# A roll along the columns of an 8192 x 8192 float32 matrix: dealing the long row pieces to the DMA engines in another order

## The chip, the core and the metric

The kernel runs on one core of a Trainium2 chip. The metric is device time in microseconds (us), the median of several executions. The core has five compute engines, which hardly matter here, and 16 DMA engines, which do all the work that counts. DMAs are put on queues by SP (SyncE), by ACT (ScalarE) and by POOL (GpSimd). Each queue feeds the same 16 DMA engines.

## The reference

```python
def setup_inputs():
    return {"x": np.random.randn(8192, 8192).astype(np.float32), "shift": 100}

def reference(x, shift):
    return np.roll(x, shift, axis=1)
```

Each row of the output is the same row of the input, turned by 100 elements: `out[r, 100:] = x[r, :8092]` and `out[r, :100] = x[r, 8092:]`. Nothing is computed; 268.4 MB are read from device memory and 268.4 MB are written to it. A row is 8192 x 4 B = 32 KiB, and rows follow one another in memory without gaps, so "rows apart" times 32 KiB gives the distance in memory.

## The kernel before

With `s = 100`, the kernel sets `a = 128` (the shift rounded up to 128 elements, so that the long writes start on a 512 B boundary of the output) and `g = a - s = 28`. Each output row is made of two pieces.

**Long pieces** (L28 to L31). Columns 128 to 8191 of the output come straight from columns 28 to 8091 of the input, 8064 elements = 32256 B of each row, by DMAs from device memory to device memory. The 8192 rows are cut into `n_chunks = 16` blocks of 512 consecutive rows, and one DMA moves one block. Even blocks are issued by SP, odd ones by ACT, so eight DMAs go on each of the two queues, in the order of the loop. The 16 completion signals of each DMA come from the 16 DMA engines; an engine has 512 / 16 = 32 rows of each DMA. Within a DMA the access pattern is 512 x 8064, and nothing in the source says which 32 rows go to which engine. That is what the change is about.

**Heads** (L48 to L70). Columns 0 to 127 of the output need the last 100 elements of the input row and its first 28. These are fetched into SBUF by POOL's DMAs, put together, and written out as 512 B pieces. There are `n_st = 2` stages of 4096 rows; in each of them partition `p` holds 32 consecutive rows, numbered by `j` (8) and `q` (`Q = 4`), so that one DMA for one `q` takes rows that are 4 apart. For `q` = 1, 2, 3 the 128 elements that straddle the border between the previous row and this one are read as one piece (L61); they hold the 28 elements at this row's start, and the 100 at the end of the row before. L62 and L65 fetch what this leaves out, VectorE copies (L63, L66) shift the pieces to their rows in `h`, and four DMAs for each stage (L70) write `h` out. All of POOL's DMAs are on POOL's queue.

The three queues start together and share the 16 DMA engines. The kernel ends when the last DMA has landed. Its end is waited for on SP (shown at L101).

Of the kernel before, what the change touches and what calls it, by code (L numbers as in the profile page):

```python
# [1 line left out]

# [4 lines left out]


@with_exitstack
def kernel(  # L10
    ctx: ExitStack,
    tc: tile.TileContext,
    x: bass.AP,
    shift: int,
    out: bass.AP,
):
    nc = tc.nc
    n_rows, n_cols = x.shape
    s = shift % n_cols
    a = -(-s // 128) * 128  # L20
    g = a - s
    P = nc.NUM_PARTITIONS
    engines = [nc.sync, nc.scalar]
    n_chunks = 16
    rows = n_rows // n_chunks


    for i in range(n_chunks):  # L28
        r = slice(i * rows, (i + 1) * rows)
        if a < n_cols:  # L30
            engines[i % 2].dma_start(out=out[r, a:], in_=x[r, g:n_cols - s])  # L31
    if a == 0:
        return


    if a > 512:
        for i in range(n_chunks):
            r = slice(i * rows, (i + 1) * rows)
            nc.gpsimd.dma_start(out=out[r, :s], in_=x[r, n_cols - s:])
            if g > 0:  # L40
                nc.gpsimd.dma_start(out=out[r, s:a], in_=x[r, :g])
        return

    Q, J = 4, 8  # L48
    n_st = n_rows // (P * Q * J)
    reads = ctx.enter_context(tc.tile_pool(name="reads", bufs=n_st))  # L50
    heads = ctx.enter_context(tc.tile_pool(name="heads", bufs=n_st))
    xt = x.rearrange("(k p j q) c -> k q p j c", q=Q, j=J, p=P)
    ot = out.rearrange("(k p j q) c -> k q p j c", q=Q, j=J, p=P)
    tiles = []
    for k in range(n_st):
        t = reads.tile([P, Q - 1, J, a], x.dtype)
        h = heads.tile([P, Q, J, a], x.dtype)
        for q in range(1, Q):
            lead = bass.AP(tensor=x.tensor, offset=(k * P * J * Q + q) * n_cols - s,
                           ap=[[J * Q * n_cols, P], [Q * n_cols, J], [1, a]])  # L60
            nc.gpsimd.dma_start(out=t[:, q - 1], in_=lead)  # L61
        nc.gpsimd.dma_start(out=h[:, Q - 1, :, :s], in_=xt[k, Q - 1, :, :, n_cols - s:])  # L62
        nc.vector.tensor_copy(h[:, :Q - 1, :, :s], t[:, :, :, :s])  # L63
        if g > 0:
            nc.gpsimd.dma_start(out=h[:, 0, :, s:], in_=xt[k, 0, :, :, :g])  # L65
            nc.vector.tensor_copy(h[:, 1:, :, s:], t[:, :, :, s:])  # L66
        tiles.append(h)
    for k, h in enumerate(tiles):
        for q in range(Q):
            nc.gpsimd.dma_start(out=ot[k, q, :, :, :a], in_=h[:, q])  # L70


# [1 line left out]
_INS = ['x', 'shift']  # L74
_OUTS = [((8192, 8192), 'float32')]

_NUMBERS = {'shift': 100}


# [26 lines left out]
```

## Time and profile before

| what | value |
|---|---|
| median of 7 runs | 835.09 us (828.78 to 840.04) |
| the profiled execution | 835.53 us |
| its span, first to last instruction | 833.7 us |
| POOL busy / VectorE busy | 16.1 us (2%) / 3.7 us (0%) |
| moved by DMA | 272.63 MB, mean 327 GB/s |
| device memory read and written | 268.44 MB each, 644 GB/s together over the span |
| long pieces, queues q1 and q10 | 4224 packets each, 132.12 MB each |
| heads, queue q0 | 2336 packets, 8.39 MB |

The profile shows instructions of the compute engines, and packets of the DMA engines by queue. The hardware queues q1 and q10 are the ones that SP and ACT issue on, q0 is POOL's. A share of a queue is the time that its packets took, divided by 16 engines times the span. In the 4224 packets of each long queue there are 4096 rows of 32256 B, and 8 x 16 completion signals, so a row is one packet. The view of stretches of the span gives for each stretch the busy share of the 16 DMA engines and the GB/s that they moved.

### The profile page before, as it was taken

Reading aid. Unit: us, or ns where it says so; the run is one execution under the profiler, and the core shown is the slowest. Engines: PE = TensorE matmul, PEld = TensorE weight load, DVE = VectorE, ACT = ScalarE, POOL = GpSimd, SP = SyncE. Lnnn points to the kernel's source line nnn. Section 1 sums busy time; section 2 is a strip of 40 time slices with the busy share of each in tenths; the row PEclk is TensorE's granted clock in tenths of the full one; section 3 lists DMA queues with packets and bytes.
Section 4 is the critical chain, followed back from the end, with each engine's and each line's share of the span. In section 5 each row is a group of like instructions: output and inputs, shape, how many; then the busy total and the mean of one; then the engine's idle time right before and its main releaser. Section 6 shows DMA issues by size and latency. Waiting matters only on the chain. (4 is left out here: it accounts for less than half of the span.)

```text
span 833.7 us, 93 instructions
## 1 busy us (share of the span) xinstructions
DVE 3.7 (0%) x4; POOL 16.1 (2%) x22
## 2 busy tenths in 40 slices
DVE  0000000000000000000000000000000000000000
POOL 3000001000010000000000000000000000000000
DMA  9999999999999999999999999999999999999996
GB/s 297 323 335 330 335 334 324 340 324 339 334 331 339 338 329 338 342 335 340 331 332 345 328 330 319 325 334 322 325 331 320 327 328 320 316 328 316 327 322 248
DMA packets 10784, 272.63 MB, mean 327 GB/s; under 512 B 544, under 2 KB 544, under 8 KB 2592
## 3 DMA queue, kind: packets, MB, share of 16 engines
q10 hardware_dynamic: 4224, 132.12, 47.4%
q1 hardware_dynamic: 4224, 132.12, 46.4%
q0 software_dynamic: 2336, 8.39, 4.8%
HBM read 268.44 MB, written 268.44 MB: 644 GB/s over the span
## 5 line engine op out<-in xcount | busy, mean ns | idle before, releaser
L70 POOL DMA_DIRECT2D out_dram<-h x8 | 6.9, 957 | 172.3 <-DMA h<-in_x_dram 145.6
L61 POOL DMA_DIRECT2D t<-in_x_dram x6 | 5.4, 912 | 0.8 <-PEq L101 0.8
L63 DVE COPY h<-t 128x2400 f32<-128x2400 f32 x2 | 2.8, 1410 | 213.2 <-DMA t<-in_x_dram 213.2
L62 POOL DMA_DIRECT2D h<-in_x_dram x2 | 1.8, 884 | 30.6 <-DMA t<-in_x_dram 30.6
L65 POOL DMA_DIRECT2D h<-in_x_dram x2 | 1.8, 884 | 29.2 <-DMA t<-in_x_dram 29.2
L66 DVE COPY h<-t 128x672 f32<-128x672 f32 x2 | 1.0, 503 | 0.0
L87 POOL MEMSET const-float32-0.0<- 128x1 f32 x1 | 0.1, 99 | 0.2 <-issue 0.2
L87 POOL MEMSET const-bfloat16-1.0<- 128x1 bf16 x1 | 0.1, 102 | 0.0
L87 POOL MEMSET const-float32-1.0<- 128x1 f32 x1 | 0.1, 99 | 0.0
L87 POOL MEMSET const-uint8-127<- 128x1 uint8 x1 | 0.1, 99 | 0.0
## 6 DMA issues: line engine op xcount, KB each, us to landing
out_dram<-in_x_dram SPq DMA_DIRECT2D x8, 16128.0 KB, 409.7
out_dram<-in_x_dram ACTq DMA_DIRECT2D x8, 16128.0 KB, 409.0
out_dram<-h POOLq DMA_DIRECT2D x8, 512.0 KB, 185.5
t<-in_x_dram POOLq DMA_DIRECT2D x6, 512.0 KB, 123.6
h<-in_x_dram POOLq DMA_DIRECT2D x2, 400.0 KB, 155.4
h<-in_x_dram POOLq DMA_DIRECT2D x2, 112.0 KB, 149.7
```

Source lines behind the costliest of these rows:

```text
L61: nc.gpsimd.dma_start(out=t[:, q - 1], in_=lead)
L62: nc.gpsimd.dma_start(out=h[:, Q - 1, :, :s], in_=xt[k, Q - 1, :, :, n_cols - s:])
L63: nc.vector.tensor_copy(h[:, :Q - 1, :, :s], t[:, :, :, :s])
L65: nc.gpsimd.dma_start(out=h[:, 0, :, s:], in_=xt[k, 0, :, :, :g])
L66: nc.vector.tensor_copy(h[:, 1:, :, s:], t[:, :, :, s:])
L70: nc.gpsimd.dma_start(out=ot[k, q, :, :, :a], in_=h[:, q])
L87: nc = _bacc.Bacc("TRN2", target_bir_lowering=False, num_devices=1)
```

## The change

The 16 long DMAs stay 16, eight for each of SP and ACT, 512 rows each, and the same bytes go to the same places. Which rows are in a DMA, and how its access pattern is laid out, is different. A row's number is read as `64 c + 4 e + j`, with `e` from 0 to 15 and `j` from 0 to 3. A DMA takes one `j`, all 16 `e`, and 32 consecutive values of `c`. Its pattern has `e` as first dimension: 16 x 32 x 8064. One engine then has one value of `e`: rows that step by 64 (2 MiB), while the next engine's rows lie 4 further on (128 KiB). SP issues `j` = 0 and 2, ACT `j` = 1 and 3. A quarter of the matrix (2048 rows) is covered by four DMAs before the next quarter begins. The heads' code is not touched; its DMAs took rows 4 apart already.

```diff
-    for i in range(n_chunks):
-        r = slice(i * rows, (i + 1) * rows)
-        if a < n_cols:
-            engines[i % 2].dma_start(out=out[r, a:], in_=x[r, g:n_cols - s])
+    xm = x.rearrange("(c e j) w -> j e c w", e=16, j=4)
+    om = out.rearrange("(c e j) w -> j e c w", e=16, j=4)
+    depth = n_rows // 64 // 4
+    for c in range(4):
+        for j in range(4):
+            if a < n_cols:
+                cs = slice(c * depth, (c + 1) * depth)
+                engines[j % 2].dma_start(out=om[j, :, cs, a:], in_=xm[j, :, cs, g:n_cols - s])
```

## The prediction, made before the changed kernel was run

> **What bounds the kernel now.** I read the busy rows of the page first, then the share of each DMA queue, then the stretches of the span, and last the waits of SP's queue. The first two views, from the page:
>
> ```profile
> DMA  9999999999999999999999999999999999999996
> GB/s 297 323 335 330 335 334 324 340 324 339 334 331 339 338 329 338 342 335 340 331 332 345 328 330 319 325 334 322 325 331 320 327 328 320 316 328 316 327 322 248
> ...
> q10 hardware_dynamic: 4224, 132.12, 47.4%
> q1 hardware_dynamic: 4224, 132.12, 46.4%
> q0 software_dynamic: 2336, 8.39, 4.8%
> HBM read 268.44 MB, written 268.44 MB: 644 GB/s over the span
> ```
>
> All 16 DMA engines are at work from the first slice to the last; the compute engines are idle. The shares give the price of a row: (47.4% + 46.4%) x 16 x 833.7 us / 8192 rows = 1.527 us for each row if the completion packets were free, counted on 32256 B. They are free (4 B each, 9 ns in the packet records). So a row costs an engine about 1.53 us, or 21.1 GB/s. The packet records give the same picture in detail: the fastest rows took 1.193 us (27.0 GB/s, 433 GB/s over 16 engines), half took over 1.47 to 1.52 us, one in twenty over 2.0 us. A row that nothing holds up takes 22% less than the mean. Something that the engines share holds them back: the memory, or the way to it.
>
> The stretches, eight of about one pair of long DMAs each (columns: length, VectorE and POOL busy, clock, DMA share, GB/s):
>
> ```profile
> 0.00:104.00 104.00, 1.83 (x2) 9.14 (x14) 1.00 0.98 323
> 312.00:416.00 104.00, 0.00 (x0) 0.00 (x0) 1.00 1.00 337
> 520.00:624.00 104.00, 0.00 (x0) 0.00 (x0) 1.00 1.00 326
> 624.00:728.00 104.00, 0.00 (x0) 0.00 (x0) 1.00 1.00 324
> 728.00:833.00 105.00, 0.00 (x0) 0.00 (x0) 1.00 0.93 310
> ```
>
> The second half moves long rows alone, and is the cleanest place: DMA share 1.00, 324 to 326 GB/s. It holds still for 200 us, so this is a steady limit and no start-up effect. In the last stretch the share is 0.93: engines run out of rows before the slowest does, and 7% of 105 us = 7 us are lost there.
>
> ```profile
> SPq L101 <- DMA out_dram<-in_x_dram: 324.4, 4, 102.9
> SPq L31 <- DMA out_dram<-in_x_dram: 47.8, 4, 17.0
> ```
>
> Issuing is not late: SP put its last long DMA in at 424.7 us, and then only waited for landings, 324.4 us in all. The median long DMA lands 409 us after its issue. About four are always queued on each ring.
>
> **The change part by part.**
>
> *Issue.* 16 long DMAs before and after, 512 rows each, 32 for each engine, the same order of SP and ACT. The instruction order on SP, ACT and POOL is the same; only the pattern turns from 512 x 8064 into 16 x 32 x 8064. If making the longer pattern costs more, the four queued DMAs (some 400 us of work) cover it. Bare price with that cover gone: the shortest issue in the trace took 0.58 us, so 8 x 0.58 = 5 us for each queue. I take 0.
>
> *Heads.* Untouched: 18 DMAs on POOL, last issued at 249 us. They hold 4.8% of the engines, 40 us of the span, wherever they run. Only their neighbours change. With the long rows out of their way or in it, they could move by some us against a slack of over 300 us to the end. I take 0.
>
> *No bytes, packets or waits change.* Everything hangs on one term: 93.8% of 833.7 = 782 us in which 16 engines copy rows. What can change is the 1.53 us of a row, since neighbouring engines read and write 128 KiB apart and not 1 MiB (if an engine had 32 consecutive rows before), an engine's next row is 2 MiB on and not 32 KiB, and the two rings work on adjacent rows and not 16 MiB apart. All 32 rows that are under way lie in 2 MiB of the input and 2 MiB of the output.
>
> The trace does not show the address of a row's packet, so this is bounded. *From below*: with no contention, 1.193/1.527 of 782 = 611 us, which saves 171. That is not reachable by an order of rows if memory itself is the limit: the Trainium skill's "HBM Reference", section Specifications, gives about 716 GB/s for the memory that a pair of cores shares, and the trace shows 644. By row alone I would allow 171 us; by the page at most (1 - 644/716) x 833.7 = 84 us, an estimate. I let the page set this end, as the steady 1.00 share at 324 GB/s (650 GB/s of reads and writes) agrees with a shared limit. *From above*: the rule that bears on the change is in "DMA: Bandwidth & Descriptors", section Latency and other measured facts, the row on HBM row pitch at large powers of two: copies between tensors with a row pitch of 512 KiB ran at 207 GB/s in each direction, of 2 MiB at 164, of 4 MiB at 103. It speaks against the change if the pitch that matters is that of one engine's list, which becomes 2 MiB: 782 x (207/164 - 1) = +205 us, an estimate. It speaks for the change if what matters is the distance between engines, which falls from 1 MiB to 128 KiB. The trace has 322 GB/s in each direction at what I take for 1 MiB, far above the rule's best, so its sizes do not carry over; and the engines drift, so that nobody steps together for long. I give it the sign in the second reading, and no size: the streams that collide are those under way at one time, and these come closer.
>
> *The size*, from the nearest row, the long-only slices. The 15 slices from the 25th to the 39th average 324 GB/s; the best has 334, the worst 316. If rows met as they do in the best slice all the time: 782 x (1 - 324/334) = -23 us. Part of this spread is chance (some 200 rows in a slice), so I take half, -12 us. The tail of 7 us I leave, since engines that finish early have the same 32 rows of each DMA afterwards.
>
> Sum: 833.7 - 12 = 822 us of span; with the 1.8 us outside the span 823.5. The profiled execution (835.53) stands 0.4 us over the median, so against the median the prediction is 823 us.
>
> **The rivals.**
>
> *A: rows get slower by crowding.* All streams now lie in 2 MiB of each tensor. If the memory spreads its work over its parts by address bits above 1 MiB, the order before used many parts and this one uses few. For it: the wide spread of row times (1.19 to over 2.0 us) shows that rows do collide singly. Against: 128 KiB is the smaller power-of-two distance[...]. It decides from a row of 1.535 us on (4.2 us x 16 / 8192 = 8 ns more). Price: at the worst long-only slice, 782 x (324/316 - 1) = +20 us, 855 us; if all rows took 1.69 us (the slowest quarter starts there): +83 us, 918 us. Likeliest within it: about 860.
>
> *B: nothing that matters changes.* If the limit is bytes per second of the memory, blind to order, or if addresses are mixed so well that any 32 streams look alike, the row stays at 1.53 us and the time at 835. It also comes out so if the hardware dealt the 512 rows in small steps before, and the change is then hardly one. For it: the steadiness of 324 to 326 GB/s, while the engines' relative places drift. Against: nothing in the profile excludes an effect of order.
>
> *C: a larger gain.* Row time falls to near the memory's own limit, and the engines end together: -60 to -84 us, 750 to 775 us. For it: the fastest quarter of rows already runs at about 1.2 us. Against: it needs nearly the full figure of the page.
>
> **How the numbers follow.** A measurement of this kernel can tell about 0.5%, 4.2 us, from no change. My case has 0.40 (its own range 805 to 831), C 0.04, B 0.17, A 0.39. Faster (0.44) is my case and C together, same (0.17) is B, slower (0.39) is A. A is nearly as likely as my case; I stay with mine because the distance between streams falls, and the only measured rule on distance says that this is the good direction. The 8-in-10 range leaves out most of C and the far part of A: 785 to 890 us.
>
> **What would show it.** Right: q1 and q10 together about 93.5% of a shorter span, so a row at 1.505 us; long-only stretches at 328 to 334 GB/s with a share of 1.00; heads' share as before. A: the same 1.00 share at under 320 GB/s, and longer landings than 409 us. B: 324 to 326 GB/s again. Wrong altogether: a share clearly under 1.00 in the middle (then issuing or dealing has failed, and not the memory), packets of another size than one for each row, or a last stretch far under 0.93, which would mean that engines got slower unevenly.

## The result: 0.8% faster, and the profile after

The changed kernel takes 828.38 us (median of 14 runs, 826.72 to 830.83) against 835.09 us of the kernel before (35 runs, 828.78 to 840.87). The ratio is 0.9924, with a 95% interval of 0.9903 to 0.9944. Ratios, here and below, and their intervals are taken from the runs within 1.5% of the fastest of their kernel, so that where times spread widely they differ from the quotient of the medians. The predicted 823 us was 5 us too low: the sign was right, and of a forecast gain of 12 us, 7 came. The profiled execution took 828.23 us with a span of 826.4 us, 7.3 us under the span before.

The page of the changed kernel: the busy rows in 40 slices, then the queues (packets, MB, share of 16 engines' time).

```profile
DMA  9999999999999999999999999999999999999996
GB/s 304 330 331 328 338 338 329 342 331 335 334 337 339 344 336 339 338 338 345 325 345 338 333 326 328 326 326 329 329 328 326 334 328 331 325 326 334 329 326 245
...
q10 hardware_dynamic: 4224, 132.12, 47.4%
q1 hardware_dynamic: 4224, 132.12, 47.2%
q0 software_dynamic: 2336, 8.39, 4.2%
HBM read 268.44 MB, written 268.44 MB: 650 GB/s over the span
```

Stretches of the changed kernel (columns as before: length, VectorE, POOL, clock, DMA share, GB/s), and the waits of SP's queue:

```profile
0.00:104.00 104.00, 1.83 (x2) 9.14 (x14) 1.00 0.98 327
312.00:416.00 104.00, 0.00 (x0) 0.00 (x0) 1.00 1.00 338
520.00:624.00 104.00, 0.00 (x0) 0.00 (x0) 1.00 1.00 330
624.00:728.00 104.00, 0.00 (x0) 0.00 (x0) 1.00 1.00 328
728.00:826.00 98.00, 0.00 (x0) 0.00 (x0) 1.00 0.93 312
```

```profile
SPq L107 <- DMA out_dram<-in_x_dram: 322.8, 4, 101.3
SPq L37 <- DMA out_dram<-in_x_dram: 47.8, 4, 16.8
```

The engines are as full as before, issuing is no later, and the long-only stretches move 328 to 330 GB/s where they moved 324 to 326. But the sum that I had made, so many rows by so many us, does not show it. A row costs (47.4% + 47.2%) x 16 x 826.4 / 8192 = 1.527 us, as before. By engine time, most of the 7.3 us is in the heads (q0: 40.0 to 34.7 us), and the rest mainly in idle time. The same profiles thus give two readings, and they had to be separated by runs.

### The profile page after: what moved, and what is told of

Same layout as the page of the kernel before. It is cut to its first block, busy times and chain, and to the rows that moved or that the text cites. A ratio compares the mean times of both kernels' runs of the same rounds, so it can differ in the third digit from the quotient of the medians.

```text
span 826.4 us, 93 instructions
## 1 busy us (share of the span) xinstructions
DVE 3.7 (0%) x4; POOL 16.1 (2%) x22
## 3 DMA queue, kind: packets, MB, share of 16 engines
q10 hardware_dynamic: 4224, 132.12, 47.4%
q1 hardware_dynamic: 4224, 132.12, 47.2%
```

## The experiments

The theories when the runs began: D, the streams of neighbouring engines come closer together; R, the two rings work on adjacent rows; S, the step of an engine's own list counts; H, the hardware dealt the rows one by one before, and not in runs of 32 as I had supposed. Ratios are to the kernel before on the same chip. There the kernel before ran at 826.5 to 828.3 us (medians) beside these runs, 1% under the 835.09 us above, so absolute times and GB/s are compared only within one chip. A ring is the queue of SP or of ACT. Where a cut of the code shows `xm` alone, `om` is `out` rearranged in the same way.

**Which distance, which rings.** First, before's distance between engines taken to the two ends.

Neighbours 1 row apart:

```diff
+    xm = x.rearrange("(i d e) w -> i e d w", e=16, d=32)
+    om = out.rearrange("(i d e) w -> i e d w", e=16, d=32)
+    for i in range(16):
+        engines[i % 2].dma_start(out=om[i, :, :, a:], in_=xm[i, :, :, g:n_cols - s])
```

> Neighbouring engines 1 row apart (32 KiB), an engine's rows step by 16 (512 KiB), the two rings 512 rows (16 MiB) apart as before. Theory D (the gain comes from bringing the streams of one ring close together): as fast as the changed kernel or faster, ratio to before 0.985 to 0.993. Theory R (the gain comes from the two rings working on adjacent rows): no gain, 0.997 to 1.003. Theory H (the hardware dealt the 512 rows of a DMA one by one before, so this is the same deal): 1.00 and the same long-only rate of 324 to 326 GB/s.

Measured: 826.28 us, ratio 0.9989 (0.9960 to 1.0018). D had asked for at least the gain of the changed kernel: closer is not better by itself. R, S and H are left. H had also asked for a long-only rate of 324 to 326 GB/s; it was 330, on a chip where the kernel before is 1% faster too.

Neighbours 512 rows apart, the same lines with:

```diff
+    xm = x.rearrange("(e i d) w -> i e d w", e=16, d=32)
```

> Neighbouring engines 512 rows apart (16 MiB), each with its own 512 consecutive rows in all, the two rings 32 rows (1 MiB) apart. Theory D: slower than before, 1.01 or more, since the streams lie 16 times further apart than before. If any distance does because addresses are well mixed: 0.995 to 1.005. Theory R: at most a little faster, 0.995 to 1.00.

Measured: 2438.63 us, ratio 2.8419 (2.8265 to 2.8573; the medians give 2.95). D had the direction; nobody had the size. Here is the page of that run:

```profile
DMA  9999999999999999999999999999999999999998
GB/s 117 123 112 124 109 114 106 118 118 115 108 114 131 112 129 128 116 120 120 124 124 118 113 113 112 122 120 107 115 108 109 114 106 118 113 119 125 107 109 95
...
q1 hardware_dynamic: 4224, 132.12, 49.9%
q10 hardware_dynamic: 4224, 132.12, 47.0%
```

All 16 engines are called busy throughout, and move a third of the bytes: (49.9% + 47.0%) x 16 x 2358.9 / 8192 = 4.46 us a row. "Busy" here means that a row is under way; how fast its bytes flow it does not tell.

The changed deal with the rings 128 MiB apart; `xm` and `om` are those of the changed kernel:

```diff
+    for c in range(2):
+        for j in range(4):
+            for h in range(2):
+                cs = slice((c + 2 * h) * 32, (c + 2 * h + 1) * 32)
+                engines[h].dma_start(out=om[j, :, cs, a:], in_=xm[j, :, cs, g:n_cols - s])
```

> The deal of the changed kernel for each DMA (neighbours 128 KiB apart, step 2 MiB), but SP works on rows 0 to 4095 and ACT on rows 4096 to 8191, so the rings are 128 MiB apart. Theory D: the gain stays, 0.990 to 0.995. Theory R: the gain is gone, 0.998 to 1.003.

Measured: 820.65 us, 0.9937 (0.9918 to 0.9956). The gain stays, so R falls: adjacent rows on the two rings are not what brings it.

Neighbours 64 rows apart, steps of one row:

```diff
+    xm = x.rearrange("(b e j d) w -> b j e d w", e=16, j=2, d=32)
+    for b in range(8):
+        for j in range(2):
+            engines[j].dma_start(out=om[b, j, :, :, a:], in_=xm[b, j, :, :, g:n_cols - s])
```

> Neighbouring engines 64 rows apart (2 MiB), an engine's rows consecutive (32 KiB on), SP's and ACT's rows of an engine 32 rows (1 MiB) apart. Theory D: a little slower than before, 1.00 to 1.01 (twice the distance). Theory S (the step of an engine's own list is what counts, 2 MiB in the changed kernel, 32 KiB here and before): no difference from before, 0.997 to 1.003.

Measured: 1489.59 us (1435.49 to 1532.85), against 826.48 of before: 1.80 times by the medians, 1.74 by the fastest run alone. S, which took 32 KiB for the step of before too, had expected no loss, and falls as it stood. This run and the one with 512 rows have the same step (32 KiB) and the same distance between the rings (1 MiB): from 2 to 16 MiB between neighbours the time grew from 1.80 to 2.95 times by the medians, so the distance costs. At 2 MiB it is so dear that 1 MiB, where I had put the kernel before, began to look doubtful.

**How the rows were dealt before.** Two runs for H. The first keeps before's pattern and only skips every second row:

```diff
+    xm = x.rearrange("(b m h) w -> b h m w", m=512, h=2)
+    om = out.rearrange("(b m h) w -> b h m w", m=512, h=2)
+    for b in range(8):
+        for h in range(2):
+            engines[h].dma_start(out=om[b, h, :, a:], in_=xm[b, h, :, g:n_cols - s])
```

> The pattern of before (512 x 8064, nothing said about engines), but a DMA takes every second row of a block of 1024: SP the even ones, ACT the odd ones. Theory B32 (the hardware gives each engine 32 consecutive entries of the first dimension): neighbouring engines are then 64 rows (2 MiB) apart as in the run with 64 rows for each engine, and the time is 1.6 to 1.9 times that of before. Theory H (it deals entry by entry): neighbours are 64 KiB apart, and the time is within 1% of before.

Measured: 820.69 us, 0.9905 (0.9876 to 0.9934). Not 1.6 to 1.9 times: the runs of 32 fall.

The second writes out what I had supposed of before, with two DMAs for each block of 512 rows:

```diff
+    xm = x.rearrange("(i e d) w -> i e d w", e=16, d=32)
+    om = out.rearrange("(i e d) w -> i e d w", e=16, d=32)
+    for i in range(16):
+        for d in (slice(0, 31), slice(31, 32)):
+            engines[i % 2].dma_start(out=om[i, :, d, a:], in_=xm[i, :, d, g:n_cols - s])
```

> What before does under theory B32, written out: engine e has rows 512 i + 32 e + d, d = 0 to 30 in one DMA (16 x 31 x 8064), and d = 31 in a second one (16 x 8064). B32: ratio to before 0.997 to 1.003. H: neighbours come to lie 1 MiB apart where they were 32 KiB apart, so the time moves, by -0.5% to +20% (2 MiB costs 80%).

Measured: 1057.83 us (1025.40 to 1121.67), ratio 1.2414 (1.2353 to 1.2475; the medians give 1.28). B32 is far off, and H's own range, up to +20%, is exceeded too. Its page, which is under that of before in every slice:

```profile
GB/s 250 282 284 275 281 271 285 272 278 275 259 275 278 280 264 260 277 277 277 250 277 265 271 266 247 258 255 271 257 250 251 267 268 263 255 260 276 271 271 204
...
q10 hardware_dynamic: 4352, 132.12, 49.1%
q1 hardware_dynamic: 4352, 132.12, 46.6%
```

Here a row took (49.1% + 46.6%) x 16 x 1023.6 / 8192 = 1.913 us. The kernel before does not behave like 1 MiB, and does behave like neighbours 1 row apart (0.9989). So the runs of 32 are out, and H fits: if the 512 x 8064 pattern is dealt entry by entry, the change moved the neighbours from 32 KiB to 128 KiB *apart*, not from 1 MiB together. The times cannot rule out small runs of rows, since the deals from 32 to 128 KiB all lie within 1% of each other; with runs of four, say, neighbours were 128 KiB apart before as well.

With H, the step of before is 512 KiB and not 32 KiB. No run has a step of 32 KiB and a short distance, so how much of the 1.24 and 1.80 against before is due to the step is not shown.

**The distance, more finely.** The changed kernel's lines with `j=16` (all 32 groups of an engine in one DMA for each `j`):

```diff
-    xm = x.rearrange("(c e j) w -> j e c w", e=16, j=4)
+    xm = x.rearrange("(c e j) w -> j e c w", e=16, j=16)
```

> The deal of the changed kernel with 16 for 4: neighbouring engines 16 rows (512 KiB) apart, an engine's next row 256 on (8 MiB), SP and ACT on adjacent rows. If the distance between neighbours has a best value near 128 KiB: 0.996 to 1.01. If a long step of an engine's list did harm: slower by several per cent, since 8 MiB is four times the step of the changed kernel. If what helps is that the step is long: 0.985 to 0.992.

Measured: 863.89 us, 1.0437 (1.0407 to 1.0467). A loss already, larger than the end of the range that a best value near 128 KiB had been given; that a longer step helps is out. "A long step does harm" had named a loss of this size. Distance and step are changed together here, and which of them costs the 4% is not shown.

With `j=2` (eight `c`, two `j`):

> The deal of the changed kernel with 2 for 4: neighbours 2 rows (64 KiB) apart, step 32 rows (1 MiB). Between the run with neighbours 1 row apart (0.9989) and the changed kernel (0.9924), so 0.993 to 0.998, if the distance acts smoothly; 0.997 to 1.001 if the gain needs 128 KiB.

Measured: 822.52 us, 0.9944 (0.9920 to 0.9969), the smooth case. Under H this is the very deal of the run with every second row, and the two intervals overlap.

Last, the changed step with before's distance:

```diff
-    xm = x.rearrange("(c e j) w -> j e c w", e=16, j=4)
+    xm = x.rearrange("(c j e) w -> j e c w", e=16, j=4)
```

> The distance of before with the step of the changed kernel: neighbouring engines 1 row apart (32 KiB), an engine's next row 64 on (2 MiB), SP and ACT 16 rows apart. If the distance between neighbours gives the gain: 0.997 to 1.002. If the step does: 0.990 to 0.995.

Measured: 823.45 us, 0.9969 (0.9938 to 1.0000). This does not decide: it lies between the two, and the interval reaches into both. How the gain of the change is split between distance and step stays open.

| neighbours apart | step of an engine | ratio to before |
|---|---|---|
| 32 KiB (before, and written out) | 512 KiB | 1, 0.9989 |
| 32 KiB | 2 MiB | 0.9969 |
| 64 KiB (two runs) | 1 MiB | 0.9944, 0.9905 |
| 128 KiB (changed; rings apart) | 2 MiB | 0.9924, 0.9937 |
| 512 KiB | 8 MiB | 1.0437 |
| 1 MiB | 32 KiB | 1.2414 |
| 2 MiB | 32 KiB | 1.74 (fastest run) to 1.80 (medians) |
| 16 MiB | 32 KiB | 2.8419 |

The rows of before are given under H. Down to 512 KiB, all but the second have a step of 16 times the distance, so the two move together. All distances are powers of two; one beside them, such as 65 rows, was not run, so whether the size of the distance costs or its being a power of two is open.

**Long rows or heads.** The heads were left out of both kernels by a `return` ahead of `Q, J = 4, 8`.

> The long pieces of before alone; the heads are left out, so columns 0 to 127 of the output stay unwritten. Theory M (the limit is bytes in and out of memory): the heads are 1.6% of the bytes, ratio 0.980 to 0.990. Theory E (the limit is engine time): the heads held 4.8% of the engines, ratio 0.950 to 0.960.

Measured: 816.53 us, 0.9891 (0.9854 to 0.9928).

> The long pieces of the changed kernel alone, heads left out as in the run before. Theory L (the long rows themselves pass faster when neighbours are 128 KiB apart): 0.7% under the run before. Theory Q (what got faster is the heads' packets, whose engine time fell from 40.0 to 34.8 us, since the long rows no longer stand in their way): the same as the run before within 0.3%.

Measured: 802.75 us, 0.9706 (0.9672 to 0.9740). On the same chip this is 13.8 us under the run before, 1.7%. The stretches, first of before's long pieces alone, then of the changed ones (length, POOL, clock, DMA share, GB/s):

```profile
104.00:312.00 208.00, 0.00 (x0) 1.00 1.00 328
312.00:520.00 208.00, 0.00 (x0) 1.00 1.00 327
520.00:728.00 208.00, 0.00 (x0) 1.00 1.00 328
```

```profile
104.00:312.00 208.00, 0.00 (x0) 1.00 1.00 333
312.00:520.00 208.00, 0.00 (x0) 1.00 1.00 332
520.00:728.00 208.00, 0.00 (x0) 1.00 1.00 333
```

And the shares of the queues in the same order:

```profile
q1 hardware_dynamic: 4224, 132.12, 49.9%
q10 hardware_dynamic: 4224, 132.12, 48.9%
```

```profile
q1 hardware_dynamic: 4224, 132.12, 49.4%
q10 hardware_dynamic: 4224, 132.12, 49.2%
```

Theory L has the direction and not the size, 1.7% for its 0.7%, and Q falls: without heads the long rows pass faster by themselves, 1.567 to 1.544 us a row by these shares. M holds over E in the first of the two runs: leaving out 40 us of engine time saved 1.1%; with the heads gone the rows took longer (1.527 us in the profile of before, 1.567 here). Engine time of the heads was not what the kernel paid for.

The heads cost 1.000 - 0.9891 = 1.1% with the old deal and 0.9924 - 0.9706 = 2.2% with the new one. So the long pieces alone gain 1.9 points, and the whole kernel 0.8. About 1.1 points are lost again when the heads are there. If ratios carry over between sets of runs (0.9924 comes from one in which the kernel before took 835 us, the other two from one in which it took 827 us), this difference is sure in sign, hardly in size.

Where they are lost is not shown. In the two profiles of the result, the rate rose less from 0 to 416 us, where heads run (332 to 334 GB/s), than from 520 to 728 us (325 to 329). On the chip of the first runs it is the other way round. There the deal with neighbours 1 row apart, then the changed deal with the rings apart:

```profile
0.00:208.00 208.00, 1.83 (x2) 12.58 (x18) 1.00 0.99 331
208.00:416.00 208.00, 1.83 (x2) 3.47 (x4) 1.00 1.00 338
520.00:728.00 208.00, 0.00 (x0) 0.00 (x0) 1.00 1.00 330
```

```profile
0.00:208.00 208.00, 1.83 (x2) 12.58 (x18) 1.00 0.98 334
208.00:416.00 208.00, 1.83 (x2) 3.47 (x4) 1.00 1.00 341
520.00:728.00 208.00, 0.00 (x0) 0.00 (x0) 1.00 1.00 331
```

Each is one execution, of kernels whose times spread by about 1%. What it is in the heads that meets the new deal worse was not tried.

**What the limit is.** The long rows on 14 engines:

```diff
-    xm = x.rearrange("(c e j) w -> j e c w", e=16, j=4)
+    full = n_rows // 56 * 56
+    xm = x[:full].rearrange("(c e j) w -> j e c w", e=14, j=4)
...
+    nc.sync.dma_start(out=out[full:, a:], in_=x[full:, g:n_cols - s])
```

> The deal of the changed kernel with 14 for 16: the long rows run on 14 engines, neighbours 4 rows apart, step 56 rows; 16 rows that are left go in a DMA of their own. Theory M (memory is the limit; 14 engines at 1.193 us a row could carry 379 GB/s): 0.985 to 1.00. Theory E (an engine takes its 1.53 us for a row whatever the others do): 16/14, so 1.10 to 1.14.

Measured: 876.69 us, 1.0604 (1.0559 to 1.0648). Outside the ranges of both theories, and between them. The page says why:

```profile
DMA  8888898888988888888888888888888887555554
GB/s 301 346 329 336 326 340 339 334 336 338 337 342 339 336 334 333 344 333 326 339 326 332 327 326 326 327 332 330 321 327 335 323 330 302 218 216 216 218 218 176
```

The stretches while all are at it, and near the end:

```profile
520.00:680.00 160.00, 0.00 (x0) 0.00 (x0) 1.00 0.87 328
740.00:860.00 120.00, 0.00 (x0) 0.00 (x0) 1.00 0.50 217
```

For 33 slices 14 engines move what 16 move, about 330 GB/s: while all are at it, the total is no smaller, as M had it. Then the share drops to a half and the rate to 217 GB/s. Eight engines are left, each at 217 / 8 = 27.1 GB/s, the 1.193 us of an unhindered row. The completion signals of the long DMA that ended last come from six engines at 727 to 740 us, and from eight at 866 to 869 us. Already in one of the first two, six came at 100 to 103 us and eight at 114 to 116 us. With equal shares of rows, six were served better all along, so the eight were late. The total is a limit of all engines together; how it is shared among them is not even. (That 14 as first dimension puts the rows on 14 engines shows in the same signals and in the share of 0.87.)

## Why the prediction was right, and where it was not

- *What bounds the kernel: right.* The engines share a limit, 328 to 330 GB/s in the long-only stretches after the change; 14 engines reach it too (328). Whether it is the memory or the way to it was left open and stays so. It is no fixed rate: 16 busy engines moved 116 GB/s with neighbours 16 MiB apart.
- *The deal before: wrong, and it is the step the sign was argued from.* I supposed that each engine had 32 consecutive rows, so 1 MiB between neighbours. The runs with every second row (0.9905) and with 1 MiB written out (1.2414) show that it had not. Dealt one by one, which fits best, the change widened the distance from 32 to 128 KiB. Had it really fallen from 1 MiB, some 20% and not 0.8% would have been gained, by the run that wrote 1 MiB out. "The distance between streams falls" was unfounded, and the right sign was luck. Rival B had named the case, and then expected no change from it.
- *The rule of the Trainium skill* ("DMA: Bandwidth & Descriptors", section Latency and other measured facts, on HBM row pitch): read by the distance between engines its direction agrees with these runs. Its fall from 207 GB/s at 512 KiB to 164 at 2 MiB is mild beside this case's, from 316 to 181 GB/s in the profiles, where the step differs too. Read by the step of an engine's list it would have cost 205 us; the changed kernel has that 2 MiB step and gained.
- *The size*: I took half of the distance between the mean and the best slice, -12 us. Measured: -7.3 us between the profiles, so it was too large by two thirds. For long pieces alone it is -13.8 us, close to the term; but the half was a guess, and no run ties the spread of the slices to the deal.
- *Heads: cost mis-sized.* I took 0, with a slack of 300 us as cover. Slack covers a wait, not a share in a common limit: leaving the heads out saved 1.1% and 2.2%. By these runs they cost 1.1 points more than with the old deal, with the reservation made there.
- *The tail*: I counted 7% of the last stretch, 7 us, as lost. In the packet records of the kernel before, 12 engines were still moving 325 GB/s between 12 and 8 us before the end, as much as all 16. Against that rate the last 8 us lose about 4 us (an estimate from the same records).
- *All rows under way within 2 MiB*: not so. The engines' signals of ACT's last long DMA after the change come from 802.3 to 825.5 us. At two rows of 1.527 us for each row of a queue that is seven to eight rows, or about 15 MiB at a step of 2 MiB (an estimate). The distances of the table are those of the lists; with long steps, rows under way are further apart.
- *What would show it*: the rate was right (328 to 330 of "328 to 334"). The row was to fall to 1.505 us and stayed at 1.527, and the heads' share was to stay and fell from 4.8% to 4.2%. A row's time is no safe measure at a shared limit: without heads it grew to 1.567 us while the kernel got shorter.
- *Rival A* (crowding) did not come, but the change did not test it, since under H it drew the streams of a ring apart. Rings 128 MiB apart gave about the same gain as on adjacent rows. The large losses lay at the other end, in streams far apart.
- *Rival C* (750 to 775 us) did not come: no order of the rows with the heads in had a median under 820 us.

## What to carry to other kernels

When a copy between device-memory tensors is at its limit, find out by a run which rows go to which engine before arguing about distances: a pattern of 512 rows was not dealt in runs of 32 here and fits dealing one by one, and patterns with 16 as first dimension behave as if each engine had its own index. With 32 KiB rows, neighbouring engines 32 to 128 KiB apart are within 1% of each other; 512 KiB (step 8 MiB) cost 4%, 1 MiB 24% and 2 MiB 74 to 80% (step 32 KiB). Judge such a kernel by GB/s in a clean stretch and not by busy shares: 16 engines at "9" were moving anything from 116 to 333 GB/s.

## What the runs showed of the hardware that had not been expected

- The order in which 16 busy engines go over the same bytes changes the rate by a factor of nearly three (330 to 116 GB/s). In lists with the same step of 32 KiB the mean rate fell from 266 GB/s at 1 MiB between neighbours to 181 at 2 MiB and 116 at 16 MiB. The first loss appears between 128 and 512 KiB, where the step grows too; the best ratios are at 64 to 128 KiB, not at the closest, by less than 1%. Why is not shown.
- Unhindered, one engine moves 27.1 GB/s (217 GB/s on eight), so 12 of them (325 GB/s at the end of the kernel before) fill what 16 get there. The surplus of engines buys no rate in this copy.
- Under the limit, engines are not served alike: with 14 engines, six were done some 130 us before the other eight.
